# Gated MLP of a hybrid decoder layer: the second product of two feature tiles goes bank by bank between the first product's products of the third tile

## The chip, the core and the metric

The kernel runs on one NeuronCore of a Trainium2 chip. The metric is the device time of one execution in microseconds (us). The engines named below are TensorE (PE in the rows; PEld is its weight load), VectorE (DVE), ScalarE (ACT), GpSimd (POOL) and SyncE (SP, which only issues DMAs here). Each of them works through its own instructions in the order in which they stand.

## What is computed

One decoder layer over 2048 tokens of 1024 features: RWKV-7 time mixing and windowed attention side by side, an output projection, and then a gated MLP with a short causal convolution. The change lies in the MLP alone:

```python
D_MODEL, SEQ, N_META, D_FF, CONV_WIDTH = 1024, 2048, 16, 2816, 3

def conv_ffn(u, w_up, conv_w, conv_b, w_down):
    hid = u @ w_up                                   # first product, 1024 -> 2 * 2816
    hid = (hid * conv_w[0] + shift_right(hid, 1) * conv_w[1]
           + shift_right(hid, 2) * conv_w[2] + conv_b)
    gate, val = jnp.split(hid, 2, axis=-1)
    return (jax.nn.silu(gate) * val) @ w_down        # second product, 2816 -> 1024
...
    h = h + concat([y_rwkv, y_attn], axis=-1) @ w_out[layer]
    u = rms_norm(h, norm2_w[layer])
    h = h + conv_ffn(u, w_up[layer], conv_w[layer], conv_b[layer], w_down[layer])
```

## The kernel before, in words

The mixers fill the first half of the span (`phase1`, which the change leaves alone). The MLP is `phase2`. It takes the tokens in three parts, twice `PARTS = [384, 384, 256]` tokens each; they are called part 0, 1 and 2 here, after the index `i`. In each part a loop goes over the 22 feature tiles `f` of 128 gate and 128 value features.

For a tile, `up_products` computes the first product by Winograd's variant of Strassen's scheme: seven products of half size, in the order p1, p2, p6, p5, p7, p3, p4. Each product is 12 matmuls (tile name `up`): four slices of the contraction, and for each three matmuls, because every operand is split into a high and a low part (`mm3`). It goes into one PSUM bank of a pool of four, so that each product takes the bank that the fourth one before it has left. ACT empties p1 into the tile `cu` (L1100); DVE adds the others up, from PSUM, into `c11`, `c12`, `c22` and `cu` (L1104 to L1120; the trace shows all but `cu` as `c`). Of `cu` and of the three others there is one buffer each, so the next tile's first evacuation waits until the convolution has read `cu`. The weights of a product are the tile `o`: in part 0 ACT makes the high half (L1073) and POOL the low half (L1074) of each; later four of the seven are fetched from DRAM (`kept`) and the rest is split. In part 0 DVE also makes the combined weights `tw` (L1062).

Then the convolution of the tile runs, for two halves `t` of the tokens and for gate and value: one ACT instruction (L998) and two on DVE (L1000, L1002), which read and write SBUF alone; then Silu on ACT (L1005), gate times value on DVE (L1006), and the split of the result into `gh` (ACT, L1008) and `gl` (POOL, L1009). `wsplit` fetches the tile's rows of `w_down` and splits them into `dh` (ACT, L156) and `dl` (POOL, L157), of which there are two buffers each.

The second product adds two feature tiles at a time to the sum `acc` in SBUF. `down` goes over blocks of 128 tokens and halves of 512 output features; each pair of these fills one PSUM bank (name `dn`, a pool of four) with six matmuls, three for each feature tile, and DVE adds the bank to `acc` (L1035). That is 12 banks in parts 0 and 1 and 8 in part 2. It stands behind the up products of the third tile, as one piece:

```python
                    elif len(grp) == 3:
                        self.down(grp[:2], acc, r0, False)
                        grp = grp[2:]
```

So a period of the loop is two tiles of up products (168 matmuls) and one second product (72 or 48). Tiles with an odd `f` have the second product ahead of them; tiles with an even `f` follow an odd tile's products directly and have the second product behind them. PE's order is the order of the program text: `mm3` issues through a queue that pins each matmul behind the one before. On DVE, ACT, POOL and SP a scheduler sets the order when the program is built, with the adds to `acc` preferred (`high_priority(DOWN)`).

Of the kernel before, what the change touches and what calls it, by code (L numbers as in the profile page):

```python
# [8 lines left out]
F32 = mybir.dt.float32  # L9
# [3 lines left out]
ALU = mybir.AluOpType  # L13
# [8 lines left out]
NFT = FF // 128  # L22
# [19 lines left out]
DOWN = 400  # L42
# [50 lines left out]
class K:  # L93
# [849 lines left out]
    def phase2(self):  # L943


        tc, nc, a = self.tc, self.nc, self.a
# [3 lines left out]
        with ExitStack() as es:  # L950
            pool = lambda name, bufs=1, **kw: es.enter_context(tc.tile_pool(name=name, bufs=bufs, reuse_waits="tile", **kw))
            up = pool("u2")
# [9 lines left out]
            wp, sp = pool("w2"), pool("s2")  # L962
# [13 lines left out]
            ops = operands(0)  # L976
            dpool = Pools(lp, up=(wp, "wraw"))
            r0 = 0
            self.begin2(0, 0, up, nw, ops)
            for i, half in enumerate(PARTS):  # L980
                N = half if i else half + 2
                nb = half // 64
                acc = []
                for b in range(nb):
                    acc.append(ac.tile([128, D], F32, tag=f"acc{b}", name=f"acc{b}"))
                    nc.sync.dma_start(acc[b], self.h2[r0 + 2 + b * 128:r0 + 130 + b * 128])
                grp = []
                for f in range(NFT):
                    gh = lp.tile([128, 2 * HMAX], F32R, tag="gh", name="gh", bufs=GHB)
                    gl = lp.tile([128, 2 * HMAX], F32R, tag="gl", name="gl", bufs=GHB)  # L990
                    cs = self.up_products(f, N, up, wp, sp, ops)
                    for t in range(2):
                        ts = []
                        for z in range(2):
                            c = cs[2 * t + z]
                            o = sp.tile([128, HMAX], F32, tag=f"t{z}", name=f"t{z}", bufs=TB)[:, 0:half]
                            j = 2 * f + z
                            A.activation(o, c[:, 2:half + 2], AF.Identity, bias=cols[:, C_CB + j:C_CB + j + 1],  # L998
                                         scale=cols[:, C_CW0 + j:C_CW0 + j + 1])
                            V.scalar_tensor_tensor(o, c[:, 1:half + 1], cols[:, C_CW1 + j:C_CW1 + j + 1], o,  # L1000
                                                   op0=ALU.mult, op1=ALU.add)
                            V.scalar_tensor_tensor(o, c[:, 0:half], cols[:, C_CW2 + j:C_CW2 + j + 1], o,  # L1002
                                                   op0=ALU.mult, op1=ALU.add)
                            ts.append(o)
                        A.activation(ts[0], ts[0], AF.Silu)  # L1005
                        V.tensor_tensor(ts[0], ts[0], ts[1], op=ALU.mult)  # L1006
                        hs = slice(t * half, t * half + half)
                        A.activation(gh[:, hs], ts[0], AF.Copy)  # L1008
                        P.tensor_tensor(gl[:, hs], ts[0], gh[:, hs].bitcast(F32), op=ALU.subtract)  # L1009
                    grp.append((gh, gl, self.wsplit(dpool, a["wdn"][f], [128, 1024], "d", RAWB, DB)))  # L1010
                    if f == NFT - 1:
                        if i == len(PARTS) - 1:
                            self.down(grp[:-1], acc, r0, False)
                            grp = grp[-1:]
                        if i < len(PARTS) - 1:
                            ops = operands(i + 1)
                            self.begin2(i + 1, r0 + 2 * half, up, nw, ops)
                        self.down(grp, acc, r0, True)
                    elif len(grp) == 3:
                        self.down(grp[:2], acc, r0, False)  # L1020
                        grp = grp[2:]
                r0 += 2 * half

    def down(self, grp, acc, r0, last):

        nc = self.nc
        for b, t in enumerate(acc):
            bs = slice(b * 128, b * 128 + 128)
            for h in range(2):
                hs = slice(h * 512, h * 512 + 512)  # L1030
                ps = self.psum.tile([128, 512], F32, tag="dn", name="dn")
                for e, (gh, gl, (wh, wl)) in enumerate(grp):
                    self.mm3(ps, gh[:, bs], gl[:, bs], wh[:, hs], wl[:, hs], e == 0, e == len(grp) - 1)
                with self.tc.high_priority(DOWN):
                    nc.vector.tensor_tensor(t[:, hs], t[:, hs], ps, op=ALU.add)  # L1035
            if last:
                nc.sync.dma_start(self.out[r0 + b * 128:r0 + b * 128 + 128], t)

    def up_products(self, f, N, up, wp, sp, ops):


        nc = self.nc
# [15 lines left out]
        def comb(x, y):  # L1058
# [3 lines left out]
            V.tensor_tensor(t, x, y, op=ALU.subtract)  # L1062
            return t

        def product(o, w):

            pool, bufs = self.oplace
            t = pool.tile([128, 2, 4, 128], F32R, tag="o", name="o", bufs=bufs)
# [9 lines left out]
            ps = self.psum.tile([128, 512], F32, tag="up", name="up")[:, 0:N]  # L1078
            xh, xl = ops[o]
            for k in range(4):  # L1080
                self.mm3(ps, hi[:, k, :], lo[:, k, :], xh[:, k, 0:N], xl[:, k, 0:N], k == 0, k == 3)
            return ps

        def tile_(tag):
# [148 lines left out]
```

## Time and profile before

| | us |
|---|---|
| three runs | 3063.3, 3070.81, 3078.51 |
| median | 3070.81 |
| profiled execution, its time | 3080.77 |
| its span | 3079.0 |
| nine periods in part 0 (1688.19 to 2153.08) | 464.89 |
| nine periods in part 1 (2266.56 to 2679.12) | 412.56 |
| nine periods in part 2 (2768.58 to 3052.15) | 283.57 |

The profile is of one execution. A row of the timeline gives start, duration, engine, line, operation, tiles (output, arrow, inputs), shape and count; in brackets the idle time of that engine just before, and what ended it. Matmuls overlap in the records: the distance between their starts is what one costs PE.

### The profile page before, as it was taken

The page shows a single profiled execution, that of the slowest core. Times are in us where ns is not written, and L with a number is a line of the kernel's source. Part 1 is how long each engine was busy: PE and PEld are TensorE (multiplying, and loading weights), DVE is VectorE, ACT ScalarE, POOL GpSimd, SP SyncE. Part 2 cuts the span into 40 slices and gives each one's busy share as a digit, 9 for nine tenths or more (in the row PEclk, how much of TensorE's full clock was granted, in tenths as well). Part 3 has the DMA queues.
Part 4 walks back from the last instruction along what each step waited for, and adds up shares of the span by engine and source line. Part 5 has one row for each costly group of instructions (what it writes and reads, how often), then busy time and mean ns, then how long its engine had stood idle before and what let it go on. Part 6 is the DMA issues. An engine that isn't in the chain of part 4 may idle for free.

```text
span 3079.0 us, 55147 instructions
## 1 busy us (share of the span) xinstructions
PE 2837.5 (92%) x19749; PEld 2400.5 (78%) x19749; DVE 2135.8 (69%) x6008; ACT 1187.5 (39%) x2758; POOL 1106.5 (36%) x1246
## 2 busy tenths in 40 slices
PE   6689899999999999999859999999899999989999
PEld 5567587777777777777538888888799999979998
DVE  5576756667666666666758777777765565577877
ACT  3344434334333334333224334343433333344443
POOL 3322311111101111121136656565544444366564
PEclk8799898989999999999969999999999999999999
DMA  6665777567676767576754434343644444466564
GB/s 217 208 218 183 219 226 227 191 175 227 185 240 179 228 192 223 176 232 194 257 200 155 161 126 161 125 164 123 242 148 158 140 147 160 142 240 234 211 220 164
DMA packets 302198, 586.43 MB, mean 190 GB/s; under 512 B 150570, under 2 KB 154266, under 8 KB 301924
## 3 DMA queue, kind: packets, MB, share of 16 engines
q1 hardware_dynamic: 301924, 582.90, 57.9%
q8 instruction: 157, 2.57, 0.3%
q14 instruction: 117, 0.96, 0.1%
HBM read 483.98 MB, written 98.79 MB: 189 GB/s over the span
## 4 chain that ended last, share of the span: by engine, by line
PE 62%; DVE 16%; DMA 10%; issue 4%; ACT 3%; SPq 2%; POOL 1%; DVEq 0%; ACTq 0%; POOLq 0%
PE up L87 16%; PE g L87 14%; PE dn L87 13%; PE o L87 5%; PE po L87 3%; DVE t L1000 3%; DMA wraw<-in_wup 2%; PE ma L87 2%; DMA w<-kept 2%; PE ps L87 2%; DVE t L1002 2%; DVE tw L1062 2%; SPq L588 2%; PE sc L87 1%; DMA nt<-nd 1%
## 5 line engine op out<-in xcount | busy, mean ns | idle before, releaser
L87 PE MATMUL up<-ah,o 128*128 128x386 f32 (+2 forms) x3696 | 871.5, 322 | 26.2 <-ACT cu L1100 13.0
L87 PEld LDWEIGHTS up<-ah,o 128*128 128x128 f32 x3696 | 645.1, 190 | 34.6 <-ACT cu L1100 17.8
L87 PE MATMUL up<-al,o 128*128 128x386 f32 (+2 forms) x1848 | 593.4, 321 | 6.5 <-DVE al L914 6.5
L87 PE MATMUL g<-xh,w 128*128 128x256 f32 x2016 | 430.4, 304 | 17.5 <-ACT w L171 6.8
L87 PEld LDWEIGHTS g<-xh,w 128*128 128x128 f32 x2016 | 339.7, 201 | 49.3 <-issue 20.0
L87 PEld LDWEIGHTS up<-al,o 128*128 128x128 f32 x1848 | 351.0, 190 | 8.5 <-DVE al L914 7.3
L87 PE MATMUL dn<-dh,gh 128*128 128x512 f32 x704 | 282.9, 402 | 33.5 <-DVE acc L1035 29.3
L1035 DVE TENSOR_TENSOR acc<-acc,dn 128x512 f32<-128x512 f32 x360 | 240.5, 681 | 98.8 <-PE dn L87 98.5
L87 PE MATMUL g<-xl,w 128*128 128x256 f32 x1008 | 303.4, 301 | 4.2 <-DVE xl L146 4.2
L1074 POOL TENSOR_TENSOR o<-wraw,o 128x512 fp32r<-128x512 f32 x198 | 275.1, 1393 | 60.0 <-ACT o L1073 35.0
L87 PE MATMUL dn<-dh,gl 128*128 128x512 f32 x704 | 279.9, 398 | 1.7 <-POOL gl L1009 1.7
L87 PE MATMUL dn<-dl,gh 128*128 128x512 f32 x704 | 279.0, 396 | 0.0
L157 POOL TENSOR_TENSOR dl<-wraw,dh 128x1024 fp32r<-128x1024 f32 x66 | 158.7, 2425 | 191.4 <-ACT dh L156 191.4
L87 PEld LDWEIGHTS g<-xl,w 128*128 128x128 f32 x1008 | 202.6, 201 | 16.7 <-issue 6.9
L1000 DVE SCALAR_TENSOR_TENSOR t<-c,cols,t 128x384 f32<-128x384 f32 (+1 forms) x198 | 162.2, 821 | 71.3 <-ACT t L998 69.8
L87 PEld LDWEIGHTS dn<-dh,gh 128*128 128x128 f32 x704 | 135.1, 192 | 70.9 <-DVE acc L1035 39.4
L1009 POOL TENSOR_TENSOR gl<-t,gh 128x384 fp32r<-128x384 f32 (+1 forms) x132 | 130.8, 991 | 160.9 <-ACT gh L1008 160.9
L593 DVE TENSOR_TENSOR tm<-nt,tt 128x60 f32<-128x60 f32 (+36 forms) x558 | 128.6, 231 | 82.2 <-DMA w<-kept 24.6
L1002 DVE SCALAR_TENSOR_TENSOR t<-c,cols,t 128x384 f32<-128x384 f32 (+1 forms) x198 | 180.6, 934 | 1.1
L677 POOL TENSOR_TENSOR sw<-S,wc 128x128 f32<-128x128 f32 x66 | 28.5, 432 | 422.8 <-DVE S L678 304.6
L998 ACT ACTIVATE t<-c,cols 128x384 f32<-128x384 f32 (+1 forms) x198 | 126.1, 668 | 112.8 <-DVE c L1117 106.7
L87 PE MATMUL g<-w,xh 128*128 128x256 f32 (+3 forms) x544 | 151.9, 362 | 13.5 <-ACT w L171 7.8
(283 smaller groups left out, 5657.8 us busy)
## 6 DMA issues: line engine op xcount, KB each, us to landing
w<-kept SPq DMA_DIRECT2D x448, 512.0 KB
o<-kept SPq DMA_DIRECT2D x176, 512.0 KB
wraw<-in_wup SPq DMA_DIRECT2D x88, 512.0 KB
kept<-o SPq DMA_DIRECT2D x88, 512.0 KB
wraw<-in_wdn SPq DMA_DIRECT2D x66, 512.0 KB
kept<-w SPq DMA_DIRECT2D x56, 512.0 KB
wraw<-in_wup SPq DMA_DIRECT2D x44, 256.0 KB
xt<-in_x SPq DMA_DIRECT2D x16, 512.0 KB
```

What stands on the lines that cost most here:

```text
L87: self._pin(self.nc.tensor.matmul(*args, **kw))
L157: nc.gpsimd.tensor_tensor(lo, raw, hi.bitcast(F32), op=ALU.subtract)
L588: nc.sync.dma_start(nt[p0:p0 + H], ndv[:, b * 32:b * 32 + 32, b * 32:b * 32 + 32])
L593: V.tensor_tensor(t, bc(nt[0:np_, s, s + 1:32], j, 1), tt[0:np_, 0:j, s:s + 1].to_broadcast([np_, j, m]), op=ALU.mult)
L677: P.tensor_tensor(sw, S, wc[:, :, c:c + 1].to_broadcast([128, 2, 64]), op=ALU.mult)
L998: A.activation(o, c[:, 2:half + 2], AF.Identity, bias=cols[:, C_CB + j:C_CB + j + 1], scale=cols[:, C_CW0 + j:C_CW0 + j + 1])
L1000: V.scalar_tensor_tensor(o, c[:, 1:half + 1], cols[:, C_CW1 + j:C_CW1 + j + 1], o, op0=ALU.mult, op1=ALU.add)
L1002: V.scalar_tensor_tensor(o, c[:, 0:half], cols[:, C_CW2 + j:C_CW2 + j + 1], o, op0=ALU.mult, op1=ALU.add)
L1009: P.tensor_tensor(gl[:, hs], ts[0], gh[:, hs].bitcast(F32), op=ALU.subtract)
L1035: nc.vector.tensor_tensor(t[:, hs], t[:, hs], ps, op=ALU.add)
L1062: V.tensor_tensor(t, x, y, op=ALU.subtract)
L1074: P.tensor_tensor(lo, w, hi.bitcast(F32), op=ALU.subtract)
```

## The change

The second product of a pair of tiles is cut into steps, one for each bank (`down_steps`). When a pair is complete, at the start of the next tile (even `f`), its steps are handed to that tile's `up_products` as `fill`. There they are issued behind the products: none behind the first two, then three a product behind the third to the sixth (two a product in part 2), none behind the seventh. The first steps stand, then, behind 36 matmuls of the tile that follows the pair. The last tiles of a part (f = 20 and 21) keep their own piece at the end. An even tile is called a fill tile from here on, an odd one a plain tile. Ten pairs of a part are treated so.

```diff
                 for f in range(NFT):
...
-                    cs = self.up_products(f, N, up, wp, sp, ops)
+
+                    fill = []
+                    if len(grp) == 2 and f < NFT - 1:
+                        fill, grp = self.down_steps(grp, acc, r0, False), []
+                    cs = self.up_products(f, N, up, wp, sp, ops, fill)
...
-                    elif len(grp) == 3:
-                        self.down(grp[:2], acc, r0, False)
-                        grp = grp[2:]
...
+    def down_steps(self, grp, acc, r0, last):
...
+        def step(b, t, h):
             bs = slice(b * 128, b * 128 + 128)
...
+            hs = slice(h * 512, h * 512 + 512)
+            ps = self.psum.tile([128, 512], F32, tag="dn", name="dn")
+            for e, (gh, gl, (wh, wl)) in enumerate(grp):
+                self.mm3(ps, gh[:, bs], gl[:, bs], wh[:, hs], wl[:, hs], e == 0, e == len(grp) - 1)
+            with self.tc.high_priority(DOWN):
+                nc.vector.tensor_tensor(t[:, hs], t[:, hs], ps, op=ALU.add)
...
+        return [lambda b=b, t=t, h=h: step(b, t, h) for b, t in enumerate(acc) for h in range(2)]
...
+        share, todo = -(-len(fill) // 5), list(fill)
+        ahead = [2]
...
             for k in range(4):
                 self.mm3(ps, hi[:, k, :], lo[:, k, :], xh[:, k, 0:N], xl[:, k, 0:N], k == 0, k == 3)
+            if ahead:
+                ahead[0] -= 1
+                if not ahead[0]:
+                    ahead.pop()
+                return ps
+            for step in todo[:share]:
+                step()
+            del todo[:share]
             return ps
```

PE, in tile f = 2 of part 0, at the end of its third product (`ah`, `al` are the operands' high and low parts; of the three banks one half is shown):

```order
 L87 MATMUL up<-al_19647,o 128x386
 L87 MATMUL up<-ah_19646,o 128x386
+L87 MATMUL dn<-dh,gh 128x512
+L87 MATMUL dn<-dl,gh 128x512
+L87 MATMUL dn<-dh,gl 128x512
...
 L87 MATMUL up<-ah_19644,o 128x386
 L87 MATMUL up<-al_19645,o 128x386
```

The fourth product now stands behind three banks of the second product; before, it stood directly behind the third.

ACT, in part 2, around the split of the `w_down` rows, which waits for the last `dn` matmul of a pair; before (`t_32200` and the two `gh` belong to the tile ahead of it, `cu<-up` to the tile behind it):

```order
L998 ACTIVATE t_32200<-cu,cols 128x256
L1008 ACTIVATE gh<-t_32188 128x256
L1005 ACTIVATE t_32200<-t_32200 128x256
L1008 ACTIVATE gh<-t_32200 128x256
L156 ACTIVATE dh<-wraw 128x1024 x2
L1100 ACTIVATE cu<-up 128x256
```

The same place now (`t_32252` and `t_32264` belong to the fill tile, the second `cu` to the plain tile behind it; L1002, L1009, L1012 and L1119 are the old L998, L1005, L1008 and L1100):

```order
L156 ACTIVATE dh<-wraw 128x1024 x2
L1084 ACTIVATE o<-wraw 128x512
L1012 ACTIVATE gh<-t_32252 128x256
L1002 ACTIVATE t_32264<-cu,cols 128x256
L1009 ACTIVATE t_32264<-t_32264 128x256
L1012 ACTIVATE gh<-t_32264 128x256
L1119 ACTIVATE cu<-up 128x256
```

The split stood behind the convolution of the tile ahead; now the end of that convolution stands between the split and the evacuation of the next tile's p1.

DVE, the same place in part 2 now, from the last adds to `acc` in the fill tile to the first sum of the plain tile (L1004 and L1006 are the old L1000 and L1002, L1010 the old L1006, L1139 and L1123 the old L1120 and L1104):

```order
L1041 TENSOR_TENSOR acc_29790<-acc_29790,dn 128x512
L1006 SCALAR_TENSOR_TENSOR t_32268<-c_32196,cols,t_32268 128x256
L1010 TENSOR_TENSOR t_32252<-t_32252,t_32256 128x256
L1139 TENSOR_TENSOR cu<-cu,up 128x256
L1004 SCALAR_TENSOR_TENSOR t_32264<-cu,cols,t_32264 128x256
L1006 SCALAR_TENSOR_TENSOR t_32264<-cu,cols,t_32264 128x256
L1010 TENSOR_TENSOR t_32264<-t_32264,t_32268 128x256
L1123 TENSOR_TENSOR c_32322<-up,cu 128x256
```

Before, this end of the convolution stood among the first three adds of the piece, and five adds stood between it and the next tile's first sum.

## Rows read from the trace of the kernel before

**Rows 1.** The page: busy time, share of the span and instructions of each engine
```profile
PE 2837.5 (92%) x19749; PEld 2400.5 (78%) x19749; DVE 2135.8 (69%) x6008; ACT 1187.5 (39%) x2758; POOL 1106.5 (36%) x1246
```

**Rows 2.** Nine periods each of parts 0, 1, 2: length, busy engines, PEclk, DMA share, GB/s
```profile
1688.19:2153.08 464.89, 432.47 (x2161) 393.95 (x2160) 355.79 (x486) 182.59 (x307) 283.04 (x216) 0.97 0.39 143
2266.56:2679.12 412.56, 412.56 (x2161) 387.20 (x2160) 249.99 (x414) 144.11 (x235) 180.17 (x216) 1.00 0.44 150
2768.58:3052.15 283.57, 281.54 (x1945) 262.52 (x1944) 224.05 (x378) 123.06 (x235) 170.86 (x216) 1.00 0.61 216
```

**Rows 3.** PE's waits in the stretch of part 0: us in total, times, longest
```profile
PE dn L87 <- DVE acc L1035: 26.6, 18, 3.2
PE up L87 <- ACT cu L1100: 5.8, 9, 1.1
```

**Rows 4.** The same by stretch: periods of part 0 (two), part 2; one second product, part 1
```profile
1741.47:1791.52 50.05, 46.97 (x241) 43.04 (x240) 39.27 (x54) 20.29 (x35) 31.93 (x24) 1.00 0.40 147
1842.45:1895.10 52.65, 49.79 (x242) 44.96 (x241) 39.59 (x54) 20.29 (x35) 32.03 (x24) 0.94 0.38 140
...
2768.58:2799.55 30.97, 30.97 (x218) 29.08 (x217) 24.11 (x42) 13.68 (x27) 18.91 (x24) 1.00 0.64 221
...
2296.07:2312.40 16.33, 16.33 (x73) 13.52 (x73) 11.46 (x20) 2.77 (x5) 3.31 (x4) 1.00 0.21 82
```

**Rows 5.** Timeline, part 0: fifth bank of the piece behind the even tile ending at 1821.84
```profile
1828.59 0.68 DVE L1035 TENSOR_TENSOR acc<-acc,dn 128x512 f32<-128x512 f32 x1
...
1829.33 0.50 PE L87 MATMUL dn<-dh,gh 128*128 128x512 f32 x1 [1.84 <-DVE acc L1035]
...
1831.86 1.37 POOL L1009 TENSOR_TENSOR gl<-t,gh 128x384 fp32r<-128x384 f32 x1 [2.05 <-ACT gh L1008]
```

**Rows 6.** Timeline, part 0, behind the odd tile whose up products end at 1806.39
```profile
1813.90 0.53 ACT L1008 ACTIVATE gh<-t 128x384 fp32r<-128x384 f32 x1 [3.42 <-DVE t L1006]
...
1814.50 1.01 POOL L1009 TENSOR_TENSOR gl<-t,gh 128x384 fp32r<-128x384 f32 x1 [1.52 <-ACT gh L1008]
```

**Rows 7.** Timeline, part 1, behind the odd tile whose up products end at 2327.15
```profile
2331.13 1.01 POOL L1009 TENSOR_TENSOR gl<-t,gh 128x384 fp32r<-128x384 f32 x1 [1.59 <-ACT gh L1008]
```

**Rows 8.** Timeline, part 2: end of a second product, start of the odd tile
```profile
2830.03 2.01 ACT L156 ACTIVATE dh<-wraw 128x1024 fp32r<-128x1024 f32 x2 [2.13 <-PE dn L87]
...
2830.51 0.28 PE L87 MATMUL up<-ah,o 128*128 128x256 f32 x1
...
2830.71 0.69 DVE L1035 TENSOR_TENSOR acc<-acc,dn 128x512 f32<-128x512 f32 x1 [0.68 <-PE dn L87]
...
2831.16 4.81 POOL L157 TENSOR_TENSOR dl<-wraw,dh 128x1024 fp32r<-128x1024 f32 x2 [2.45 <-ACT dh L156]
...
2834.81 1.48 DVE L1000 SCALAR_TENSOR_TENSOR t<-c,cols,t 128x256 f32<-128x256 f32 x1 [0.73 <-ACT t L998]
...
2836.29 2.54 POOL L1074 TENSOR_TENSOR o<-wraw,o 128x512 fp32r<-128x512 f32 x2
...
2836.55 2.56 DVE L1002 SCALAR_TENSOR_TENSOR t<-c,cols,t 128x256 f32<-128x256 f32 x1
...
2840.22 0.41 DVE L1117 TENSOR_TENSOR c<-up,c 128x256 f32<-128x256 f32 x1
```

**Rows 9.** Timeline, part 2: convolution behind that odd tile, evacuation of the next p1
```profile
2842.04 0.48 DVE L1000 SCALAR_TENSOR_TENSOR t<-c,cols,t 128x256 f32<-128x256 f32 x1
...
2842.22 0.60 ACT L998 ACTIVATE t<-cu,cols 128x256 f32<-128x256 f32 x1
...
2845.11 0.42 ACT L1008 ACTIVATE gh<-t 128x256 fp32r<-128x256 f32 x1 [2.29 <-DVE t L1006]
...
2845.61 0.74 POOL L1009 TENSOR_TENSOR gl<-t,gh 128x256 fp32r<-128x256 f32 x1 [1.22 <-ACT gh L1008]
2845.96 0.40 ACT L1005 ACTIVATE t<-t 128x256 f32<-128x256 f32 x1
2846.27 0.36 ACT L1100 ACTIVATE cu<-up 128x256 f32<-128x256 f32 x1
```

More of the change, by code (lines that the diff above doesn't have):

```diff
@@ L1018, in phase2, with up_products @@
                         self.down(grp, acc, r0, True)
-                    elif len(grp) == 3:
-                        self.down(grp[:2], acc, r0, False)
-                        grp = grp[2:]
                 r0 += 2 * half
     def down(self, grp, acc, r0, last):
+        for step in self.down_steps(grp, acc, r0, last):
+            step()
+    def down_steps(self, grp, acc, r0, last):
         nc = self.nc
-        for b, t in enumerate(acc):
+        def step(b, t, h):
             bs = slice(b * 128, b * 128 + 128)
[L1029 to L1036, printed above, removed]
+            hs = slice(h * 512, h * 512 + 512)
[4 more added lines that the diff above has]
+                nc.vector.tensor_tensor(t[:, hs], t[:, hs], ps, op=ALU.add)
+            if last and h:
                 nc.sync.dma_start(self.out[r0 + b * 128:r0 + b * 128 + 128], t)
-    def up_products(self, f, N, up, wp, sp, ops):
+        return [lambda b=b, t=t, h=h: step(b, t, h) for b, t in enumerate(acc) for h in range(2)]
+    def up_products(self, f, N, up, wp, sp, ops, fill):
         nc = self.nc
@@ L1081, in product @@
                 self.mm3(ps, hi[:, k, :], lo[:, k, :], xh[:, k, 0:N], xl[:, k, 0:N], k == 0, k == 3)
+            if ahead:
[4 more added lines that the diff above has]
+            for step in todo[:share]:
+                step()
+            del todo[:share]
             return ps
```

## The prediction

> **What bounds the kernel now.** First the page: PE is busy 92% of the span [rows 1], so only its idle time and its half-speed time can be won. Then the busy time by stretch, for nine periods of each part of the MLP [rows 2]. Part 1 has no idle time at all: PE is busy 412.56 us of 412.56, and a period is 45.84 us. Part 2 is idle 2.03 us of 283.57; a period is 31.51 us on average, 30.97 where nothing waits [rows 4]. Part 0 is idle 32.4 us of 464.89, at a mean clock of 0.97; a period is 51.65 us. So part 0 is what the change can better, and parts 1 and 2 can hardly get better, only worse.
>
> What one matmul costs follows from rows 4: a second product of part 1 is 72 matmuls in 16.33 us, 0.227 each, 1.36 a bank. The rest of a period of part 1, 29.51 us, is 168 up matmuls, 0.176 each, 2.11 a product. In part 0 (386 columns for 384) a product is 2.12 us, a tile 14.83, and a period without any wait would be 16.33 + 2 x 14.83 = 46.0 us. In part 2 it is (30.97 - 8 x 1.36) / 14 = 1.43 us a product and 10.04 a tile. Part 0 is thus 5.65 us a period over its floor, of which 3.6 are waits. PE's waits there name two causes [rows 3]: 26.6 us in which a `dn` matmul waits for an add to `acc`, and 5.8 us in which the fifth up product waits for its bank, which `cu` empties. The timeline shows the first [rows 5]: the fifth bank starts 1.84 us late, as the add of the first bank stands on DVE behind convolution instructions. The remaining 2 us a period are start-up behind a wait and clock: a period at granted clock 1.00 takes 50.05 us with 3.08 idle, one at 0.94 takes 52.65 with 2.86 [rows 4].
>
> **Removed: the wait for the adds.** Three banks between two products leave DVE 6 us and more for three adds of 0.68 [rows 5], and PE comes back to a bank only after a product. This wait goes, and the convolution has the whole tile to run in. The `cu` wait of the even tiles goes too: six banks now stand between p1 and p7 of a fill tile. The number of matmuls, adds, splits and bytes is unchanged; PE's order is pinned by the program, so the banks do go where the text puts them.
>
> **Added in all parts: a wait for `gl`.** The first bank reads the output of the plain tile just ahead. Before, 84 up matmuls covered its making; now 36 do. Its last matmul wants `gl` at the end of the plain tile's products plus three products and five matmuls: 7.49 us in part 0, 7.46 in part 1, 5.42 in part 2. Behind odd tiles `gl` was ready 9.12 us after the products in part 0 (1815.51 less 1806.39) [rows 6], 4.99 in part 1 [rows 7] and 5.80 in part 2 (2846.35 less 2840.55, the period's start plus a tile) [rows 8, 9]. So the price is 1.6 us in part 0, nothing in part 1 and 0.4 in part 2, if a plain tile runs as an odd one did. It does not quite: an odd tile began with DVE idle; a plain tile begins with the end of the fill tile's convolution. The even tile is the other bound: it had a whole convolution ahead of it, and two adds, and its `gl` came after 11.39 us [rows 5], 3.9 too late. For part 0 I take 2.8, between the two, as the plain tile inherits about half a convolution. Waits fall from 3.6 to 2.8 us a period; with start-up and clock in proportion the excess falls from 5.65 to 4.4. Ten periods: -12.5 us; with 1.6 it is -31, with 3.9 it is +5. For part 2 the bounds are 0.4 and, with the same lag at 256 columns for 384 (2.27 x 2/3), 1.9; I take 0.7.
>
> **Added in part 2: a wait for the plain tile's `cu`.** The split of the `w_down` rows hangs on the last `dn` matmul. Let T be the start of the product behind the last bank (2830.51 in rows 8). ACT starts `dh` 0.5 us before T, POOL runs `dl` from T + 0.65 to T + 5.46 [rows 8]. Before, the convolution was over by then. Now its end stands there: on DVE one instruction of L1002, the product of the halves, the last sum of `cu`, and L1000 and L1002 on `cu`; then Silu, another product, `gh`, and only behind that, on ACT, the evacuation of the plain tile's p1. Queued behind it on ACT are the plain tile's other steps, on DVE its first sum, and on PE p7, which needs p1's bank at T + 5 x 1.43 = T + 7.17.
>
> The rows show what DVE's SBUF instructions cost beside POOL: L1000 at 2834.81 takes 1.48 us instead of 0.48 [rows 8, 9] and ends 0.32 behind `dl`; instructions that read PSUM keep their 0.41 [rows 8]. So: add over at T + 1.3 (convolution instructions stand ahead of it), L1002 held by the first `dl` to T + 3.4, product 0.41 and last sum 0.41 to T + 4.2, ACT 0.60 to T + 4.8, L1000 held by the second `dl` to T + 5.8, L1002 held by the `o` split of 1.27 behind it to T + 7.1, Silu 0.40, product 0.41, `gh` 0.42, `cu` 0.36 [rows 9]: T + 8.7, with some 0.05 us for each hand-over T + 9.2. PE waits 2.0 us. If nothing held DVE, the same chain would end near T + 5.6 and cost nothing; if another `o` split went ahead, as at 2836.55, where L1002 sat out two of them (2.56 us) [rows 8], it is 3.3. I take 2.0: the chain needs only one blocking by each POOL instruction in its way.
>
> Whether POOL holds DVE up is thus the hinge. The Trainium skill ("SBUF — State Buffer", section "Who interferes with whom") says that a VectorE instruction with two SBUF inputs and a GpSimd instruction that reads SBUF exclude each other for a whole instruction, and that the one that issues first holds the other up. That speaks against this change, and the 1.48 us agree. By that rule alone L1002 at 2836.55 should have run between the two splits; the row shows it behind both. By the rule the wait would be the 2.0 us taken; by that row it would be the 3.3.
>
> The waits of a period of part 2 are then 2.0 + 0.7 = 2.7 us. A wait cost 1.3 times its length in the period at full clock (50.05 - 46.0 over 3.08) [rows 4], so 3.5 us, less the 0.54 that a period now has over 30.97: +3.0 a period, +30 us for ten. The ends are 0 and +62.
>
> **Part 1.** The same chain with instructions half as long again ends about a microsecond later, T + 10.2, and p7 wants the bank at T + 10.5. It just fits; one more POOL instruction in the way (1.27 to 2.4 us) makes it a wait of 1 to 2. I take 0.2 a period with its start-up: +3 us, from 0 to +20. In part 0 the need is T + 10.6, and a miss there lies inside the bounds above. The new SP order moves some loads of `o` and of raw weights past each other; the buffers hold four to six products ahead, and no `up` matmul waited for a load in these stretches [rows 2, 3], so I take nothing for it.
>
> **Sum.** -12.5 + 3 + 30 = +20 us. On the profiled execution, 3080.77 us, that is 3101; that execution stands 10 us over the median of the runs, so against the median of 3070.81 the forecast is 3091.
>
> **Rivals.** (1) DVE keeps ahead of POOL, because L1002 gets in before the first `dl` (it is a matter of 0.6 us at T + 0.65), and the chain ends before T + 7.17. Then part 2 and part 1 cost nothing and part 0 gives 20 to 31: about 3045, faster than before. It is decided by whether `cu` is empty by T + 7.17 in part 2. Against it stand the 4.81 us of `dl`, unbroken, in just that stretch. (2) Only the first `dl` holds DVE: waits of 1.0 + 0.4 in part 2, 1.3 x 1.4 - 0.54 = +1.3 a period, +13, which cancels part 0: 3071. (3) DVE loses more often: part 0 at its upper end (+5), part 1 at 1.5 us a period (+15), part 2 at 3.5 (+35): 3125. For it speaks the 2.56 us row; against it that most such rows are nearer one POOL instruction.
>
> **How the numbers follow.** The forecast's case (3080 to 3105) has a chance of 0.45, rival 1 0.17, rival 2 0.25, rival 3 0.13. About half a per cent, 15 us, is what a measurement of this kernel can tell from no change. Faster by more than that is rival 1, 0.17; within it rival 2 and the low edge of the forecast, 0.25 + 0.06 = 0.31; slower the rest, 0.52. The range for 8 in 10 leaves out the better part of rival 1 and the worse half of rival 3: 3050 to 3122.
>
> **What would show it.** In part 0 the waits for `acc` (26.6 us) are gone, a `dn` matmul waits for `gl` or `gh` once a period, 2 to 4 us, and a period is near 50.4 us. In part 2 an up matmul waits some 2 us for `cu` in each plain tile, L1000 or L1002 takes over 1 us beside `dl`, and a period is near 34.5. Part 1 stays within 0.5 us of 45.84. I am wrong if part 2 keeps 31.5 us a period (POOL did not hold DVE up), or if part 0 stays at 51 or more (the wait was only moved).

## The result and the profile after

The changed kernel takes 3099.03 us (median; 3093.84 to 3101.95), the kernel before 3072.59 beside it. The ratio is 1.0091, with a 95% interval of 1.0067 to 1.0115: slower by 0.9%. The profiled execution has a span of 3100.2 us, 21.2 over that of before.

The nine periods of each part stand here as in [rows 2], from one start of a plain tile to another, with the same work done before each of them. The columns are the stretch, its length, the busy time of PE, PEld, DVE, ACT and POOL with their instructions, the granted clock of PE, the DMA share and GB/s:

```profile
1686.09:2148.08 461.99, 429.13 (x2161) 391.14 (x2161) 385.48 (x486) 181.94 (x306) 285.89 (x217) 0.99 0.39 144
2259.62:2673.39 413.77, 413.77 (x2162) 387.11 (x2162) 270.31 (x414) 141.19 (x234) 181.23 (x217) 1.00 0.46 149
2763.41:3070.91 307.50, 288.00 (x1946) 267.93 (x1945) 229.23 (x379) 120.02 (x235) 173.04 (x217) 0.98 0.59 201
```

Against [rows 2], part 0 is 2.9 us shorter, part 1 1.2 longer, part 2 23.9 longer (one profiled execution each). What lies between these stretches follows from their edges: ahead of the first -2.1, between parts 0 and 1 -1.9, between 1 and 2 +0.6, behind the last +2.4. That is +21.2 in all. So the loss is in part 2, and part 0 gave almost nothing.

PE's waits in parts 0 and 2 (engine, tile and line, the releaser; us in total, times, longest) name the places. Part 1 has none:

```profile
PE up L87 <- DVE c L1129: 17.2, 9, 1.9
PE dn L87 <- ACT gh L1012: 11.7, 7, 1.7
PE dn L87 <- POOL gl L1013: 3.2, 9, 0.4
...
PE up L87 <- ACT cu L1119: 19.5, 9, 2.2
```

The 26.6 us for the adds of [rows 3] are gone from part 0. In their place stand 1.9 us a period in which p1 of a fill tile waits for a PSUM bank (DVE's sum of p5, L1129, empties it), 0.35 us a period for `gl`, and in seven of the nine periods 1.7 us for `gh`, all at the first bank of `dn`. That is 32.1 us in nine periods, where the waits of [rows 3] were 32.4. Part 2 has 2.2 us a period for `cu`.

The timeline of part 2 behind one T (2795.48, the first row of PE: the start of the product behind the last bank) shows where `cu` was:

```profile
2795.48 0.28 PE L87 MATMUL up<-ah,o 128*128 128x256 f32 x1
...
2796.14 2.43 POOL L157 TENSOR_TENSOR dl<-wraw,dh 128x1024 fp32r<-128x1024 f32 x1 [2.53 <-ACT dh L156]
...
2796.42 2.43 DVE L1006 SCALAR_TENSOR_TENSOR t<-c,cols,t 128x256 f32<-128x256 f32 x1
...
2798.85 2.61 POOL L157 TENSOR_TENSOR dl<-wraw,dh 128x1024 fp32r<-128x1024 f32 x1
...
2799.10 0.41 DVE L1139 TENSOR_TENSOR cu<-cu,up 128x256 f32<-128x256 f32 x1
...
2800.25 1.50 DVE L1004 SCALAR_TENSOR_TENSOR t<-cu,cols,t 128x256 f32<-128x256 f32 x1 [0.73 <-ACT t L1002]
...
2801.43 1.47 POOL L1085 TENSOR_TENSOR o<-wraw,o 128x512 fp32r<-128x512 f32 x1
...
2801.79 1.40 DVE L1006 SCALAR_TENSOR_TENSOR t<-cu,cols,t 128x256 f32<-128x256 f32 x1
...
2804.55 0.36 ACT L1119 ACTIVATE cu<-up 128x256 f32<-128x256 f32 x1
...
2804.97 0.40 PE L87 MATMUL up<-ah,o 128*128 128x256 f32 x1 [2.17 <-ACT cu L1119]
```

Three DVE instructions of the convolution, 0.48 us each where POOL has no split running [rows 9], take 2.43, 1.50 and 1.40. The first two end 0.3 us behind a `dl`, the third 0.3 us behind an `o` split of 1.47. After them ACT empties p1, and p7, which needs that bank, starts 2.17 us late. The Trainium skill ("SBUF — State Buffer", section "Who interferes with whom") says that a VectorE instruction with two SBUF inputs contends with a GpSimd instruction that reads SBUF for a port pair that the two share, as an exclusive lock. The trace agrees in the main: each of the three ends only behind POOL's split, and the second `dl` starts at 2798.85, where L1006 ends. The rows are not cleanly apart, though: L1010 (gate times value, two SBUF inputs, 0.41 us from 2798.77) reaches 0.3 us into the second `dl`, which takes 2.61 us for 2.43.

### The profile page after: what moved, and what is told of

Same layout as the page of the kernel before. It is cut to its first block, busy times and chain, and to the rows that moved or that the text cites. A ratio compares the mean times of both kernels' runs of the same rounds, so it can differ in the third digit from the quotient of the medians.

```text
span 3100.2 us, 55131 instructions
## 1 busy us (share of the span) xinstructions
PE 2838.4 (92%) x19749; PEld 2398.0 (77%) x19749; DVE 2196.6 (71%) x6008; ACT 1180.5 (38%) x2758; POOL 1115.2 (36%) x1246
## 4 chain that ended last, share of the span: by engine, by line
PE 65%; DVE 17%; DMA 7%; ACT 4%; issue 4%; SPq 3%; POOL 1%; DVEq 0%; ACTq 0%; POOLq 0%
PE up L87 18%; PE dn L87 14%; PE g L87 13%; PE o L87 5%; DVE t L1004 3%; PE po L87 3%; DVE t L1006 3%; PE ma L87 2%; SPq L588 2%; PE ps L87 2%; DMA w<-kept 1%; DMA nt<-nd 1%; PE sc L87 1%; PE pt L90 1%; DVE tw L1070 1%
## 5 line engine op out<-in xcount | busy, mean ns | idle before, releaser
L87 PE MATMUL up<-ah,o 128*128 128x386 f32 (+2 forms) x3696 | 894.9, 324 | 57.4 <-ACT cu L1119 25.5
L87 PEld LDWEIGHTS up<-ah,o 128*128 128x128 f32 x3696 | 653.3, 192 | 72.7 <-ACT cu L1119 28.1
L157 POOL TENSOR_TENSOR dl<-wraw,dh 128x1024 fp32r<-128x1024 f32 x66 | 172.5, 2626 | 63.7 <-ACT dh L156 63.7
L1002 ACT ACTIVATE t<-c,cols 128x384 f32<-128x384 f32 (+1 forms) x198 | 125.9, 667 | 179.1 <-DVE c L1136 168.5
L1084 ACT ACTIVATE o<-wraw 128x512 fp32r<-128x512 f32 x198 | 121.6, 625 | 175.8 <-PE up L87 155.4
L1006 DVE SCALAR_TENSOR_TENSOR t<-c,cols,t 128x384 f32<-128x384 f32 (+1 forms) x198 | 175.2, 898 | 1.5
L1004 DVE SCALAR_TENSOR_TENSOR t<-c,cols,t 128x384 f32<-128x384 f32 (+1 forms) x198 | 145.8, 746 | 42.2 <-ACT t L1002 39.6
L1009 ACT ACTIVATE t<-t 128x384 f32<-128x384 f32 (+1 forms) x132 | 64.6, 489 | 269.3 <-DVE t L1006 269.2
```

The lines of the kernel that those rows point to most:

```text
L87: self._pin(self.nc.tensor.matmul(*args, **kw))
L157: nc.gpsimd.tensor_tensor(lo, raw, hi.bitcast(F32), op=ALU.subtract)
L1084: A.activation(hi, w, AF.Copy)
```

## Experiments

Theory A: in part 2 POOL's `dl` holds the end of the fill tile's convolution, and so `cu`. All time lost is there; the waits of part 0 are matters of their own. The rivals are named with each run. Line numbers of these kernels shift by a few.

### One part alone

`e1_parts01` asks for `i < 2` beside `len(grp) == 2`, `e2_part2` for `i == 2`; the other parts keep the old piece:

```diff
-                    if len(grp) == 2 and f < NFT - 1:
+                    if i < 2 and len(grp) == 2 and f < NFT - 1:
...
                         self.down(grp, acc, r0, True)
+                    elif len(grp) == 3:
+                        self.down(grp[:2], acc, r0, False)
+                        grp = grp[2:]
```

> The banks go between the products in parts 0 and 1 only; part 2 keeps its second product in one piece. Theory A (the loss comes from part 2 alone, part 0 gains a little): a period of part 2 is back at 31.5 us, parts 0 and 1 keep 51.3 and 46.0 us a period, and the time is some 5 us under the kernel before, near 3067 us, ratio 0.998. Rival B (the loss is spread over the program, by load order or clock): part 2 stays above 32.5 us a period, or the time is over 3080 us.

> The banks go between the products in part 2 only; parts 0 and 1 keep their pieces. Theory A: parts 0 and 1 are those of the kernel before, a period of part 2 is 34.2 us with one wait of 2.1 us for cu in each plain tile, and the time is 25 to 28 us over the kernel before, near 3099 us, ratio 1.0085. Rival B: part 2 alone costs under 12 us, and the time is under 3085 us.

Measured: 0.9977 (0.9956 to 0.9998) and 1.0084 (1.0053 to 1.0116). The nine periods of parts 0 and 2 in `e1_parts01`, by stretch as above:

```profile
1679.09:2139.58 460.49, 435.41 (x2161) 397.80 (x2161) 384.73 (x486) 181.94 (x306) 285.99 (x217) 0.97 0.40 144
...
2754.61:3039.76 285.15, 282.31 (x1946) 262.76 (x1944) 226.56 (x378) 122.94 (x235) 170.21 (x216) 1.00 0.62 215
```

Part 2 in `e2_part2`, the same view:

```profile
2762.40:3070.10 307.70, 288.19 (x1946) 268.15 (x1945) 228.97 (x379) 119.77 (x235) 172.96 (x217) 0.98 0.59 200
```

As theory A said, the loss comes with part 2 (307.7 against 285.2). That parts 0 and 1 together gain a little rests on the ratio of `e1_parts01` alone, whose interval just leaves out 1. Part 0 of `e2_part2`, which keeps the old piece, is no longer than that of the changed kernel (461.99):

```profile
1685.85:2147.59 461.74, 430.78 (x2161) 393.76 (x2160) 355.12 (x486) 182.58 (x307) 285.56 (x216) 0.98 0.40 144
```

From its end to the start of part 1's stretch it is 111.14 us (113.48 before, 111.54 in the changed kernel). So the old part 0 differs by 5.5 us between two traces, and what the change gains there is not shown by them.

### Without dl in part 2

`e3_no_dl` passes `i < 2` as `low`:

```diff
         hi = pool.tile(shape, F32R, tag=tag + "h", name=tag + "h", bufs=wb)
+        nc.scalar.activation(hi, raw, AF.Copy)
+        if not low:
+            return hi, hi
         lo = pool.tile(shape, F32R, tag=tag + "l", name=tag + "l", bufs=wb)
-        nc.scalar.activation(hi, raw, AF.Copy)
         nc.gpsimd.tensor_tensor(lo, raw, hi.bitcast(F32), op=ALU.subtract)
```

> As the changed kernel, but in part 2 the low half dl of the w_down rows is left out: the two GpSimd instructions of 2.4 us each are gone, and the matmuls that read dl read dh again; nothing else differs. Theory A (GpSimd's dl holds VectorE's convolution up, which makes the evacuation of the next p1 late): the waits for cu in nine periods fall from 19.5 us to under 3, a period of part 2 is 31.2 us or less, and the time is 26 to 30 us under the changed kernel, 3069 to 3073 us. Rival B (the dh split of 2.0 us on ScalarE, or the length of the chain, makes cu late): at least 12 us of the wait stay, and the time is above 3085 us.

Measured: 0.9990 (0.9969 to 1.0012), 3075.15 us. Part 2 by stretch:

```profile
2759.44:3047.73 288.29, 282.16 (x1946) 261.27 (x1945) 209.39 (x379) 122.31 (x235) 127.29 (x198) 1.00 0.64 214
```

And PE's only wait there:

```profile
PE dn L87 <- POOL gl L1015: 6.1, 9, 0.7
```

The wait for `cu` is gone, though `dh` is still there. But leaving `dl` out also moved ACT's order: the evacuation of p1 now stands ahead of the convolution's last `gh`, where in the changed kernel it stands behind it. The timeline behind T = 2790.02:

```profile
2795.37 0.37 ACT L1121 ACTIVATE cu<-up 128x256 f32<-128x256 f32 x1
...
2796.84 0.42 ACT L1014 ACTIVATE gh<-t 128x256 fp32r<-128x256 f32 x1 [0.26 <-DVE t L1012]
```

What each of the two is worth can be estimated from the rows. Without `dl`, but behind that `gh`, p1's bank would be empty at some 2797.5, 0.3 to 0.4 us late for p7 (T + 7.17 = 2797.2). With `dl`, but directly behind Silu (which ends at 2803.6 in the changed kernel), it would be empty at 2803.9, still 1.1 us late. So POOL's `dl` makes `cu` late: 1.1 to 1.8 of the 2.17 us go with it alone. The rest takes the order on ACT besides, which no run changed alone. Rival B falls. What the expectation missed by 0.8 us a period is the new row: with PE no longer held inside the plain tile, `gl` comes 0.7 us too late at the end of it.

### Eight banks behind the third product in part 2

This is `e4_part2_behind_third`:

```diff
-        share, todo = -(-len(fill) // 5), list(fill)
+        share, todo = 8 if len(fill) == 8 else 3, list(fill)
```

> As the changed kernel, but in part 2 all eight banks stand behind the third product (share 8 for 2); parts 0 and 1 are untouched. The split of the w_down rows then becomes ready three products, 4.3 us, earlier against the end of the tile, so dl (4.8 us from 0.65 us behind the last bank) is over before the last product ends at 5.7 us. Theory A: the wait for cu goes, a period of part 2 is 31.0 to 31.5 us and the time is near 3072 us, ratio 0.997 to 1.001. Rival B (a second product among the first products costs part 2 something in any place, by banks of PSUM or by gl): a period stays above 32.5 us, the time above 3082 us. Should the last banks wait for the adds to acc, that would show as a wait on L1041.

Measured: 1.0033 (1.0016 to 1.0050), a period of 33.43 us. The waits of part 2:

```profile
PE dn L87 <- POOL gl L1013: 9.2, 8, 1.2
PE dn L87 <- ACT gh L1012: 2.9, 6, 1.3
PE up L87 <- ACT cu L1119: 0.4, 1, 0.4
```

The wait for `cu` is gone, as theory A said, but the time is not: `gl` and `gh` are late by up to 1.2 and 1.3 us. Here the expectation was wrong, and by its bound (over 32.5 us a period) rival B holds for this place.

### Part 0: a later start, another division of PSUM

In part 0 of the changed kernel the same hold stands at the end of the fill tile (the plain tile that begins at 1737.26 and the start of the fill tile behind it):

```profile
1735.82 5.37 POOL L157 TENSOR_TENSOR dl<-wraw,dh 128x1024 fp32r<-128x1024 f32 x2 [2.50 <-ACT dh L156]
...
1738.86 2.74 DVE L1004 SCALAR_TENSOR_TENSOR t<-cu,cols,t 128x384 f32<-128x384 f32 x1 [0.85 <-POOL dl L157]
...
1748.91 1.78 DVE L1070 TENSOR_TENSOR tw<-wraw 128x512 f32<-128x512 f32 x1
...
1753.85 0.55 DVE L1129 TENSOR_TENSOR c<-up,cu 128x386 f32<-128x386 f32 x1
...
1754.55 0.42 PE L87 MATMUL up<-ah,o 128*128 128x386 f32 x1 [1.91 <-DVE c L1129]
```

`cu` is in time for p7 there (it is emptied from 1745.07 us, and part 0 has no wait for it), but DVE starts the plain tile's sums only behind it. The four combined weights `tw` stand in DVE's order ahead of the sum of p5, beside POOL's `o` splits (1.51, 1.03, 1.78 and 1.76 us), and so that sum comes late for the next tile's p1.

For `e6_part0_later`:

```diff
+        if N % 128:
+            share, ahead = 4, [3]
```

`e7_part0_later_up5` also gives `dn2` three banks and `up2` five.

> As the changed kernel, but in part 0 the twelve banks stand four each behind the fourth, fifth and sixth product, so that the first bank stands one product (2.12 us) later and the last one where it was. Theory A (part 0 has two waits of their own, each taken from where it stands): the wait for gh and gl of 2.0 us a period goes, the wait of the next p1 for the bank of p5 (1.9 us, L1129) stays, a period of part 0 is 49.0 us, the time some 20 us under the changed kernel, near 3079 us. Rival B (VectorE's chain through the whole period sets 51.2 us, and PE only waits for it in one place or another): a period stays above 50.5 us.

> As the kernel before this one in the list, and PSUM is divided five banks for up and three for dn in place of four and four, so that a product takes the bank of the fifth product before it. Theory A: the wait for p5's bank in part 0 goes too (p6's bank is empty 6 us earlier) and p7 wants its bank in part 2 one product, 1.4 us, later: a period of part 0 is 46.5 to 48 us, the wait for cu in part 2 is 0.7 us for 2.1, the time 3040 to 3055 us. Rival B: VectorE's chain sets the period, part 0 stays above 50 us. Three banks for four behind a product may bring back a wait for the adds: it would show on L1041, 0.3 to 1 us each.

Measured: 0.9997 (0.9978 to 1.0017) and 1.0107 (1.0070 to 1.0143). Part 0 of `e6_part0_later` by stretch:

```profile
1696.06:2133.77 437.71, 421.05 (x2161) 387.51 (x2161) 376.80 (x486) 180.92 (x306) 282.64 (x217) 1.00 0.41 152
```

PE's waits in it:

```profile
PE up L87 <- DVE c L1131: 15.1, 9, 1.7
PE dn L87 <- POOL gl L1013: 1.5, 9, 0.2
```

The longest of PE's four waits in part 0 of `e7_part0_later_up5`:

```profile
PE dn L87 <- DVE acc L1041: 22.7, 9, 2.5
```

The later start took the wait for `gh` away and left the other: 48.63 us a period, so theory A holds and PE is not just following DVE. With five banks no wait for p5's bank is left, and in part 2 the wait for `cu` fell to 0.8 us, as expected, but four banks of `dn` in a row on three buffers wait 2.5 us for the adds: 52.48 us a period. The expectation had that at 1 us at most. How much of the wait for p5's bank only hides behind this one, the run does not show.

### What makes DVE late in part 0

`e8_no_dl_part0` leaves `dl` out as above, in part 0 alone. In `e9_o_low_on_act`:

```diff
-                P.tensor_tensor(lo, w, hi.bitcast(F32), op=ALU.subtract)
+                A.activation(lo, w, AF.Copy)
```

> As the changed kernel, but the low half dl of the w_down rows is left out in part 0 (matmuls that read dl read dh); parts 1 and 2 are untouched. Theory A (dl holds up the end of the fill tile's convolution in part 0 as in part 2; cu is read out late, and from there VectorE lags through the plain tile until the bank of p5): the wait on L1129 goes, the wait for gh and gl gets under 1 us, a period of part 0 is 46.5 to 48.5 us, the time 25 to 40 us under the changed kernel. Rival B (VectorE's own load in part 0, the four combined weights of a tile beside GpSimd's splits of o, makes it late): a period stays above 50 us.

> As the changed kernel, but the low half of every o is written by ScalarE as a copy (0.62 us) and not by GpSimd as a difference (1.29 us), which leaves the subtraction out; dl stays on GpSimd. Theory A (dl is what holds VectorE up): the wait for cu in part 2 stays over 1 us, and in part 0 at least one wait of 1 us stays, a period there over 48 us. Rival B (the o splits hold VectorE up): L1070 falls from 1.2 us to 0.7, the waits of part 0 go, a period there is under 47.5 us, and the wait for cu in part 2 falls under 0.8 us.

Measured: 0.9949 (0.9930 to 0.9969) and 0.9953 (0.9930 to 0.9975). Part 0 of `e8_no_dl_part0` by stretch:

```profile
1678.13:2103.59 425.46, 420.02 (x2162) 388.00 (x2161) 354.84 (x486) 180.98 (x306) 226.41 (x199) 1.00 0.42 156
```

Part 0 of `e9_o_low_on_act`, the same view:

```profile
1671.14:2086.04 414.90, 414.90 (x2162) 389.41 (x2161) 297.63 (x486) 239.35 (x432) 95.97 (x91) 1.00 0.44 160
```

PE's only wait in part 2 of `e9_o_low_on_act`:

```profile
PE up L87 <- ACT cu L1119: 28.2, 9, 3.1
```

Without `dl` a period of part 0 is 47.27 us, without the `o` differences on POOL 46.10 and PE never waits. Leaving out `dl` is enough: in the plain tiles of `e8_no_dl_part0` the four `tw` still stand ahead of the sum of p5 (three of them now ahead of the first sum), and its bank is in time. `e9_o_low_on_act` has no wait either, so theory A may be too narrow for part 0; but there DVE's order moved too, and all four `tw` (6.1 us in the changed kernel) stand behind that sum. That the `o` splits by themselves keep the lag up is thus argued and not shown. In part 2, with the `o` splits off POOL, the wait for `cu` is still there, and in its timeline L1006 and L1004 take 2.42 and 1.50 us beside `dl`, as in the changed kernel; so theory A holds there. That the wait grew to 3.1 us is not `dl`: four `o` copies of 0.61 us each, two of them the added ones, stand on ACT ahead of `gh` and the evacuation.

### Other places for the banks

`e10_later_0_and_2` has part 0 as in `e6_part0_later` and, in part 2, all eight banks behind the fourth product; `e11_part0_six` has six each behind the fourth and fifth product in part 0 besides; `e12_combined` is `e6_part0_later` with part 2 as a piece.

> As the changed kernel, with part 0 as in e6_part0_later (four banks behind the fourth, fifth and sixth product) and in part 2 all eight banks behind the fourth product. In part 2 the first bank wants gl at 4 x 1.43 + 1.1 = 6.9 us behind the plain tile, where e4_part2_behind_third had it ready at 6.6 to 7.0; dl runs from 0.65 to 5.5 us behind the last bank, three products (4.3 us) before the tile ends, so the end of the convolution stays clear of all but its last 1.2 us. Theory A: the waits for cu and gl of part 2 are both under 0.5 us, a period there is 31.0 to 31.4 us, a period of part 0 48.6, and the time 3035 to 3045 us, ratio 0.988 to 0.991. Rival B (in part 2 something is always late when the banks stand among the products): a period of part 2 stays above 32.5 us, the time above 3055 us.

> As the kernel before this one in the list, but in part 0 six banks each stand behind the fourth and fifth product, so that the split of w_down becomes ready one product (2.12 us) earlier. Theory A (dl at the end of the tile is what makes VectorE late in the plain tile): L1004 on cu in part 0 falls from over 2 us to 1.5 or less, the wait of 1.7 us for the bank of p5 goes, a period of part 0 is 46.5 to 47.5 us, the time 10 to 20 us under the kernel before in the list. Rival B: six banks in a row wait for their adds, as the whole piece did: a wait on L1041 of 1 to 2 us a period takes the place of the other, and the period stays at 48 to 49 us.

> The two gains that stood alone, together: part 0 as in e6_part0_later (four banks each behind the fourth, fifth and sixth product), part 1 as in the changed kernel, part 2 with its second product in one piece. Theory A (the parts don't act on each other): a period of 48.6 us in part 0, 46.0 in part 1, 31.6 in part 2; the ratio is that of e1_parts01, 0.9977, less 0.009 for part 0, so 0.986 to 0.991, some 3035 us. Rival B: one of the gains is lost beside the other, and the ratio is above 0.994.

Measured: 0.9938 (0.9916 to 0.9960), 1.0021 (1.0002 to 1.0040) and 0.9910 (0.9895 to 0.9925). The first was to give 31.0 to 31.4 us a period in part 2 and gives 33.49, which lies within rival B's bounds, as its time does (3059.89 us). Its `gl` is late for another reason, the timeline behind a plain tile of part 2:

```profile
2814.24 0.63 ACT L1088 ACTIVATE o<-wraw 128x512 fp32r<-128x512 f32 x1 [3.45 <-DMA wraw<-in_wup]
...
2816.19 0.91 POOL L1013 TENSOR_TENSOR gl<-t,gh 128x256 fp32r<-128x256 f32 x1
...
2817.15 0.50 PE L87 MATMUL dn<-dh,gl 128*128 128x512 f32 x1 [1.18 <-POOL gl L1013]
```

ACT stands at an `o` copy until its raw weights have landed, and `gh` (2814.77 us) is queued behind that copy, `gl` behind an `o` split on POOL. In `e4_part2_behind_third` an `o` copy waits 1.2 us for its raw weights at the same place. Why that load comes late with these placements stays open.

In `e11_part0_six` a period of part 0 is 50.94 us, over the range of either theory. Theory A had expected an earlier `dl` to miss the convolution. It meets the convolution's first instruction instead:

```profile
1775.33 4.82 POOL L157 TENSOR_TENSOR dl<-wraw,dh 128x1024 fp32r<-128x1024 f32 x2 [6.00 <-ACT dh L156]
...
1778.32 2.25 DVE L1004 SCALAR_TENSOR_TENSOR t<-c,cols,t 128x384 f32<-128x384 f32 x1 [0.78 <-ACT t L1002]
```

The wait for p5's bank did go, but p3 now waits for the bank of p2, whose sum (L1127 in this kernel) stands on DVE behind three of the `tw`, and in four of nine periods there are 1.2 us for an add:

```profile
PE up L87 <- DVE c L1127: 19.2, 9, 2.2
```

So the lag was moved to an earlier bank. `e12_combined` has the periods that were expected, 48.78, 45.98 and 31.65 us; its ratio is the upper end of its range.

### The last banks behind the last product

This is `e13_last_behind_p4`:

```diff
-        share, todo = -(-len(fill) // 5), list(fill)
-        ahead = [2]
+        share, todo = -(-len(fill) // 4), list(fill)
+        ahead = [3]
```

> As the changed kernel, but in all parts the banks stand behind the fourth to the seventh product (three each in parts 0 and 1, two each in part 2). The first bank wants gl one product later, and behind the last product p4 stand three banks (4.1 us) or two (2.7 us): the end of the convolution (last sum, ScalarE 0.6, L1004 and L1006 0.5 each: some 2.3 us in part 2) runs there, before the split of w_down becomes ready, and dl falls beside the next tile's first sums, which read PSUM. Theory A (dl only hurts where it meets the convolution's end): the wait for cu in part 2 goes, a period there is 31.0 to 31.6 us; in part 0 the waits for gh and for the bank of p5 go, a period is 46.3 to 48.5 us; the time is 3020 to 3045 us, ratio 0.982 to 0.990. Rival B (VectorE is late wherever dl stands, in part 0 for its combined weights): a wait for tw or o, or for a bank, of over 1 us a period stays in part 0, a period is above 49.5 us, and the ratio is above 0.993.

Measured: 3020.9 us, ratio 0.9846 (0.9825 to 0.9866), faster than the kernel before by 1.5%. Nine periods of each part by stretch:

```profile
1673.96:2096.13 422.17, 418.95 (x2161) 388.04 (x2160) 369.88 (x487) 179.90 (x307) 279.79 (x216) 1.00 0.43 157
2206.16:2619.80 413.64, 413.64 (x2162) 387.09 (x2160) 272.82 (x414) 142.01 (x235) 176.98 (x216) 1.00 0.45 149
2710.16:2989.64 279.48, 279.48 (x1945) 261.98 (x1944) 206.14 (x379) 118.78 (x235) 168.00 (x217) 1.00 0.64 221
```

The only wait of PE in these stretches is in part 0:

```profile
PE dn L87 <- POOL gl L1013: 3.2, 9, 0.4
```

The timeline of part 2 around T = 2803.32, which is here the start of the next tile's p1:

```profile
2802.76 0.48 DVE L1004 SCALAR_TENSOR_TENSOR t<-cu,cols,t 128x256 f32<-128x256 f32 x1
...
2803.28 0.84 DVE L1006 SCALAR_TENSOR_TENSOR t<-cu,cols,t 128x256 f32<-128x256 f32 x1
...
2803.98 5.00 POOL L157 TENSOR_TENSOR dl<-wraw,dh 128x1024 fp32r<-128x1024 f32 x2
...
2805.06 0.36 ACT L1119 ACTIVATE cu<-up 128x256 f32<-128x256 f32 x1
```

The two banks behind p4 give the convolution's end the time that it needs. L1004 takes its 0.48 us, `dl` starts 0.1 us before L1006 ends, and ACT empties p1 into `cu` from T + 1.7 us, where p7 wants that bank at T + 4 x 1.43 = T + 5.7; in the changed kernel it was T + 9.1, with p7 a product later. Here too the evacuation stands on ACT ahead of the convolution's last `gh` (at 2806.73 us), whose input, made by L1010, is still held by `dl` (1.51 us for 0.41). Behind that `gh` it would have begun at T + 3.8, still in time. A period is 46.91, 45.96 and 31.05 us; the floors worked out ahead were 46.0, 45.84 and 30.97. `dl` is as long as ever (5.00 us for the two): it only stands elsewhere. In part 0 the first banks stand a product later as well; that alone gave 48.63 us a period (`e6_part0_later`), and the rest comes with the new places. L1004 on `cu` takes 1.22 us there on the mean, 2.18 in the changed kernel, and no p1 waits for the bank of p5; DVE's order has its part in that, as only one `tw` is left ahead of p5's sum. With 31.05 us in part 2, rival B of `e4_part2_behind_third` and `e10_later_0_and_2`, that the banks cost something there in any place, falls. This kernel beats both others.

## Why the prediction was right, and where it was not

The forecast was 3091 us (3101 for the profiled execution), slower than before; measured are 3099.03 and 3101.95. The sum was right partly by luck: the misses went opposite ways. A part's figure here takes its nine periods and the stretch behind them (with part 1 taking none):

| term | forecast | measured |
|---|---|---|
| part 0 | -12.5 | -2.9 - 1.9 = -4.8 |
| part 1 | +3 | +1.2 |
| part 2 | +30 | +0.6 + 23.9 + 2.4 = +26.9 |
| ahead of the nine periods of part 0 | not in the sum | -2.1 |
| sum | +20 | +21.2 |

The -2.1 and the -4.8 are within what traces of one and the same text differ by: with the same text ahead of it, the first stretch starts at 1686.09 us in the changed kernel and at 1679.09 in `e1_parts01`, and part 0 of `e2_part2`, the old piece, is 5.5 us shorter than before.

**The wait for `cu` in part 2: right, step by step.** The chain was to have L1006 held by the first `dl` to T + 3.4, L1004 by the second to T + 5.8, the next L1006 by an `o` split to T + 7.1, and to end by T + 9.2. With T = 2795.48 the rows above end at T + 3.4, 6.3, 7.7 and 9.4. The wait was 2.17 us for 2.0, and `e3_no_dl` shows that it goes with `dl`, all but the part that ACT's order has in it. Rival 1 fell at its hinge: L1006 started 0.28 us after `dl`, not before. The row with two splits sat out ([rows 8], 2.56 us), by which the wait would have been 3.3 us, has no counterpart: in the nine periods no L1004 or L1006 takes over 2.43 us. That sums which read PSUM keep their 0.41 us beside POOL was right as well, but the row named for it (2840.22 in [rows 8]) stands behind POOL's splits; the row of L1139 above, 0.41 us within the second `dl`, shows it.

**The wait for `gl` in part 2: right in size, but hidden.** 0.7 us were forecast, none measured, as the 2.17 us in the middle of the plain tile leave ACT and POOL time to catch up. Taking the one wait away uncovers the other: 0.7 us in `e3_no_dl`. The two should not have been added up.

**The price of a wait in part 2.** The forecast put 1.3 times its length. A period where the clock stays at 1.00 is 33.52 us, 2.55 over the 30.97 of [rows 4], for 2.17 of waiting; in four of nine periods a stretch at half clock follows, and they take about 35. The mean, 34.17, is 3.2 over 30.97, or 1.5 times. That made up, by luck, for the `gl` that did not come, and 34.5 was near.

**Part 0: the step that failed.** The term of -12.5 was mis-sized. The waits for the adds went, as forecast, and the wait for `gh` and `gl` is 2.0 us where both show, 1.7 on the mean (2.8 were put, between 1.6 and 3.9). But the working looked for what DVE's leftover convolution delays only at `gl`; it also delays the sum of p5, whose bank the next tile's p1 takes directly, and nothing was set down for that. It costs 1.9 us a period. So the waits stayed at 3.6 us a period (32.4 us before, 32.1 now) instead of falling to 2.8, and a period came to 51.3 us, where the prediction itself had named 51 or more as the sign that the wait was only moved. `e6_part0_later` shows the two waits as separate, `e8_no_dl_part0` that the one at the bank goes with `dl`. What the four `tw` ahead of p5's sum add, and the `o` splits beside them, no run changed alone. The `dl` chain was costed for parts 2 and 1, and for part 0 only its end at `cu` was looked at and left to the bounds; `cu` is in time there, and it was not the only thing behind the chain.

**Part 1** lost 1.2 us in nine periods and has no wait, as worked out: `cu` just fits. What the 1.2 us are is not shown.

## What to carry to other kernels

When work is moved between two pieces of other work, follow every step that becomes ready at its end: here the split of the next weights, which ran on another engine and held the chain that frees the next PSUM bank. Choose the place of the last piece by what its end releases: with two or three banks behind the last product, the same interleaving gained 1.5% where it had lost 0.9%. And where one engine lags, price each of the buffers that it has yet to free, not the nearest one alone, and do not add up waits that stand one behind the other. Each of these edits also let the scheduler move instructions of the other engines: compare their orders too before a wait is put down to what the edit took away.

## What the runs showed of the hardware

DVE instructions that read two SBUF operands were held by POOL's splits: in the changed kernel's rows above L1006, L1004 and L1006 start while a split runs and end 0.28 to 0.29 us behind it, after 2.43, 1.50 and 1.40 us for 0.48. A sum that reads PSUM (L1139) takes 0.41 us beside `dl`; in the trace of before L1104, from 2833.65 us, takes 0.43 beside the `dl` of [rows 8].

The granted clock fell after some waits of the same length and not after others. These are two periods of part 2 in the changed kernel, by stretch:

```profile
2763.41:2796.93 33.52, 31.36 (x218) 29.10 (x217) 25.44 (x43) 13.31 (x27) 19.31 (x25) 1.00 0.62 204
2796.93:2831.89 34.96, 32.79 (x218) 30.62 (x217) 25.42 (x43) 13.40 (x27) 19.09 (x25) 0.95 0.57 196
```

And the 3.6 us behind the wait for `cu`, in the first of them and in the second:

```profile
2771.44:2775.00 3.56, 3.56 (x29) 3.56 (x30) 3.30 (x7) 1.48 (x3) 3.51 (x5) 1.00 0.81 259
2804.97:2808.60 3.63, 3.63 (x18) 3.63 (x19) 2.84 (x7) 1.47 (x3) 3.46 (x5) 0.53 0.54 214
```

After the same 2.17 us PE does 29 matmuls in one stretch, at 2.4 GHz (1.00), and 18 in the other, near 1.2 GHz (0.53). It costs 1.4 us of the period. In part 0 of `e1_parts01` a slower clock cost nothing: two periods of it,

```profile
1747.49:1798.65 51.16, 48.72 (x240) 44.55 (x241) 42.74 (x55) 20.22 (x34) 31.78 (x24) 0.97 0.39 144
...
2054.53:2105.70 51.17, 47.20 (x240) 43.01 (x241) 42.75 (x55) 20.22 (x34) 31.77 (x24) 1.00 0.39 144
```

take 51.16 us at 0.97 with PE idle for 2.4, and 51.17 at 1.00 with PE idle for 4.0. The slow matmuls fill the time that PE would have waited for `gh`. So a missing row in the list of waits is no proof that a wait is gone: the length of the period has to be read with it.
